# Interleaved rotary embedding on one core: two of the fifth load's sixteen positions come as fp32 over the SP queue

## The chip, the cores and the metric

The kernel runs on one core of one Trainium2 chip. The metric is the device time of one execution in microseconds, the median of several runs of the same program. Profiles are single executions taken by the hardware profiler; their times count from the start of the profiled span. The core has five engines, each with an instruction queue of its own, and they meet only at semaphores: TensorE (PE), VectorE (DVE), ScalarE (ACT), GpSimd (POOL) and SyncE (SP). TensorE isn't used here. Data moves between HBM and the on-chip memory, SBUF, by 16 DMA engines. A transfer is issued by an instruction on the POOL queue or on the SP queue; in the profile q0 (software_dynamic) carries those from POOL and q1 (hardware_dynamic) those from SP.

## The reference

`x` has the shape (8, 2048, 16, 64) in fp32: batch, sequence, heads, head dimension. `cos` and `sin` are (2048, 32). Neighbouring elements of the head dimension form a pair, and each pair is rotated by the angle of its position:

```
x_pairs = x.reshape(batch, seq_len, num_heads, head_dim // 2, 2)
x1 = x_pairs[..., 0]
x2 = x_pairs[..., 1]
out1 = x1 * cos - x2 * sin
out2 = x1 * sin + x2 * cos
out = np.stack([out1, out2], axis=-1).reshape(batch, seq_len, num_heads, head_dim)
```

All arrays are fp32. `x` and `out` have 67.1 MB each.

## The kernel before

**Tiling.** A batch `b` is one tile: 128 partitions, each with K = 16 consecutive positions, each position with 16 x 64 = 1024 elements. In HBM a partition's share is 64 KB in one piece, in SBUF 32 KB, since tiles are bf16. Loads on the POOL queue cast from fp32 to bf16 on the way, and stores on it cast back. Five tile buffers (`NX = 5`) go round for the eight batches.

**Computing.** `rotate` (L61 to L80) makes three VectorE instructions for a range of positions: `qt` = x times the sine table (L74), x = x times the cosine table in place (L75), and x = x plus `qt` with the elements of each pair swapped (L80). The tables `s_tab` and `c_tab` are bf16, made once from the raw fp32 tables by three instructions (L93 to L95); the sine table holds its sign. For `b = 0` the rotation is done in two parts, of 4 and of 12 positions; later tiles are rotated whole.

**Order.** The order on each queue is written out by hand (`manual_schedule`), and semaphores come from what each instruction reads and writes. On the POOL queue stand, one behind the other: the last 12 positions of load 0 (L85), the two raw tables (L86, L87), loads 1 to 4 (L89), store 0 (L59), the mark (L106), store 1, load 5, store 2, load 6, store 3, load 7, stores 4, 5 and 6, and the first 12 positions of store 7 (L112). Load 5 reuses tile 0's buffer and waits until store 0 has landed; loads 6 and 7 wait likewise for stores 1 and 2. The mark is a GpSimd copy of one element, position 15 of tile 4, into a place that nobody reads. It makes the POOL queue wait until load 4 has landed, before store 1 is issued.

**Both ends.** The first four positions of load 0 come in fp32 over the SP queue into `head` (L84), and ScalarE casts them into tile 0 (L91). The last four positions of store 7 are cast to fp32 by ScalarE into `tail` (L118), and SP stores them (L119). Ahead of that cast ScalarE copies one element (L117) into tile 6, which makes it wait until store 6 has landed. SP's queue thus holds two transfers, and ScalarE two casts and that copy.

**Homes.** `cos_sb` and `sin_sb`, the raw tables, have a place of their own each in the pool `consts`. `qt`, `head` and `tail` share one place in the pool `stage`.

Of the kernel before, what the change touches and what calls it, by code (L numbers as in the profile page):

```python
# [2 lines left out]

# [4 lines left out]


@with_exitstack  # L10
def kernel(
    ctx: ExitStack,
    tc: tile.TileContext,
    x: bass.AP,
    cos: bass.AP,
    sin: bass.AP,
    out: bass.AP,
):
    nc = tc.nc
    fp32 = mybir.dt.float32  # L20
    bf16 = mybir.dt.bfloat16
    mult = mybir.AluOpType.mult
    add = mybir.AluOpType.add

    B, S, H, D = x.shape
    P = 128
    K = S // P
    KP = 16
    D2 = D // 2
    HD = H * D  # L30
    NX = 5
    HEAD = 4
    TAIL = 4


    x_t = x.rearrange("b (p k) h d -> b p k (h d)", p=P, k=K)
    out_t = out.rearrange("b (p k) h d -> b p k (h d)", p=P, k=K)
    cos_t = cos.rearrange("(p k) c -> p (k c)", p=P, k=K)
    sin_t = sin.rearrange("(p k) c -> p (k c)", p=P, k=K)

    consts = ctx.enter_context(tc.tile_pool(name="consts", bufs=1))
    xpool = ctx.enter_context(tc.tile_pool(name="xpool", bufs=NX))
    stage = ctx.enter_context(tc.tile_pool(name="stage", bufs=1))

    cos_sb = consts.tile([P, K * D2], fp32)
    sin_sb = consts.tile([P, K * D2], fp32)
    c_tab = consts.tile([P, K, D], bf16)
    s_tab = consts.tile([P, K, D], bf16)

    mark = consts.tile([1, 1], bf16)  # L50
    tiles = {}

    def load(b, k0=0):
        if b not in tiles:
            tiles[b] = xpool.tile([P, K, HD], bf16, name="xt")
        nc.gpsimd.dma_start(out=tiles[b][:, k0:], in_=x_t[b, :, k0:])  # L56

    def store(b, k1=K):
        nc.gpsimd.dma_start(out=out_t[b, :, :k1], in_=tiles[b][:, :k1])  # L59

    def rotate(b, k0, k1):  # L61
        nk = k1 - k0
        xp = tiles[b][:, k0:k1]
        qt = stage.tile([P, KP, HD], bf16, name="qt", tag="work")

        def rows(a):
            return a.rearrange("p k (h e) -> p k h e", h=H, e=D)

        def tab(a):
            return dataclasses.replace(  # L70
                a, offset=a.offset + k0 * D, ap=[a.ap[0], [D, nk], [0, H], [1, D]]
            )

        nc.vector.tensor_tensor(out=rows(qt[:, :nk]), in0=rows(xp), in1=tab(s_tab), op=mult)  # L74
        nc.vector.tensor_tensor(out=rows(xp), in0=rows(xp), in1=tab(c_tab), op=mult)  # L75
        q_swap = dataclasses.replace(
            qt, offset=qt.offset + 1, ap=[qt.ap[0], [2, nk * HD // 2], [-1, 2]]
        )
        x3 = xp.rearrange("p k (a j) -> p (k a) j", j=2)
        nc.vector.tensor_tensor(out=x3, in0=x3, in1=q_swap, op=add)  # L80

    with tc.manual_schedule():
        head = stage.tile([P, TAIL, HD], fp32, name="st", tag="work")
        nc.sync.dma_start(out=head[:, :HEAD], in_=x_t[0, :, :HEAD])  # L84
        load(0, HEAD)  # L85
        nc.gpsimd.dma_start(out=cos_sb, in_=cos_t)  # L86
        nc.gpsimd.dma_start(out=sin_sb, in_=sin_t)  # L87
        for b in range(1, NX):
            load(b)  # L89

        nc.scalar.copy(out=tiles[0][:, :HEAD], in_=head[:, :HEAD])  # L91
        s2 = s_tab.rearrange("p k (i j) -> p (k i) j", j=2)
        nc.vector.tensor_copy(out=s2[:, :, 0], in_=sin_sb)  # L93
        nc.vector.tensor_scalar_mul(s2[:, :, 1], sin_sb, -1.0)  # L94
        nc.vector.tensor_copy(  # L95
            out=c_tab.rearrange("p k (i j) -> p (k i) j", j=2),
            in_=cos_sb.to_broadcast([P, K * D2, 2]),
        )
        for b in range(B):
            if b == 0:  # L100
                rotate(b, 0, HEAD)
                rotate(b, HEAD, KP)
            else:
                rotate(b, 0, KP)
            if b == 1:
                nc.gpsimd.tensor_copy(out=mark, in_=tiles[NX - 1][:1, K - 1, :1])  # L106
            if b < B - 1:
                store(b)

            if b >= 1 and b - 1 + NX < B:  # L110
                load(b - 1 + NX)
        store(B - 1, K - TAIL)  # L112

        tail = stage.tile([P, TAIL, HD], fp32, name="st", tag="work")
        nc.scalar.copy(out=tiles[B - 2][:1, 0, :1], in_=tiles[B - 1][:1, K - 1, :1])  # L117
        nc.scalar.copy(out=tail, in_=tiles[B - 1][:, K - TAIL :])  # L118
        nc.sync.dma_start(out=out_t[B - 1, :, K - TAIL :], in_=tail)  # L119


# [1 line left out]
_INS = ['x', 'cos', 'sin']  # L123
_OUTS = [((8, 2048, 16, 64), 'float32')]


# [23 lines left out]
```

## Time and profile before

| what | value |
|---|---|
| median of 3 runs | 317.34 us (317.24 to 317.46) |
| span of the profiled execution | 315.5 us |
| VectorE busy | 210.4 us, 67% of the span, 30 instructions |
| ScalarE busy | 8.6 us, 4 instructions |
| GpSimd busy | 11.9 us, 23 instructions |
| HBM read, written | 67.63 MB, 67.11 MB: 427 GB/s over the span |
| VectorE waiting for loads (L74) | 28.5 us, 3 times, the longest 12.6 |
| rotation instructions, whole tile | 8.69 us each, 7 of each line |
| casts of 128x4096 on ScalarE (L91, L118) | 3.60 us each |

A group of instructions in the profile is told by its line, engine, operation and operands, `out<-in`. The timeline gives the start and the length of each in us, and in brackets how long its engine was idle before it and what ended that. The profile counts a DMA's bytes at the place that it writes, so a casting load counts half of what it reads. A transfer's DMA work consists of packets, one for each partition's piece; with 128 partitions and 16 engines each engine has 8 of a transfer, and a completion write of 4 bytes behind them.

### The profile page before, as it was taken

What the parts mean: (1) busy time and instruction counts of PE and PEld (TensorE: products, weight loads), DVE (VectorE), ACT (ScalarE), POOL (GpSimd) and SP (SyncE); (2) the same over time, 40 slices, a digit from 0 to 9 for tenths busy, and PEclk for the clock granted to TensorE, in tenths of its full rate; (3) what the DMA queues carried; (4) which work ended last, traced back from release to release, by engine and by line L of the source; (5) the groups of instructions that cost most, each with busy time, mean ns of one, the idle gap of its engine ahead of it and who ended that gap; (6) DMA issues with size and microseconds to landing.
All of it is one profiled execution on the core that took longest, in us unless ns stands there. A gap on an engine that the chain in (4) does not pass through costs nothing.

```text
span 315.5 us, 125 instructions
## 1 busy us (share of the span) xinstructions
DVE 210.4 (67%) x30; ACT 8.6 (3%) x4; POOL 11.9 (4%) x23
## 2 busy tenths in 40 slices
DVE  0009999999999999999879960799509994000000
ACT  1030000000000000000000000000000000000400
POOL 5000000000000201010000100000000000000000
DMA  7999999999999999999999999999999999999997
GB/s 252 263 282 199 199 224 241 199 199 258 208 199 266 399 482 449 399 332 245 220 399 407 386 204 199 415 515 266 199 266 465 399 399 498 432 399 407 430 432 326
DMA packets 2752, 102.24 MB, mean 324 GB/s; under 512 B 320, under 2 KB 320, under 8 KB 448
## 3 DMA queue, kind: packets, MB, share of 16 engines
q0 software_dynamic: 2464, 98.04, 96.7%
q1 hardware_dynamic: 288, 4.19, 3.4%
HBM read 67.63 MB, written 67.11 MB: 427 GB/s over the span
## 4 chain that ended last, share of the span: by engine, by line
another core or an unknown queue 88%; DMA 5%; ACT 1%; ACTq 1%; issue 0%
DMA st<-in_x_dram 5%; ACT xt L91 1%; ACTq L145 1%; ACT xt L117 0%; ACTq L117 0%
## 5 line engine op out<-in xcount | busy, mean ns | idle before, releaser
L74 DVE TENSOR_TENSOR qt<-xt,s_tab 128x16384 bf16<-128x16384 bf16 (+2 forms) x9 | 69.7, 7743 | 28.6 <-DMA xt<-in_x_dram 28.5
L75 DVE TENSOR_TENSOR xt<-xt,c_tab 128x16384 bf16<-128x16384 bf16 (+2 forms) x9 | 69.7, 7743 | 0.4
L80 DVE TENSOR_TENSOR xt<-xt,qt 128x16384 bf16<-128x16384 bf16 (+2 forms) x9 | 69.7, 7744 | 0.3
L93 DVE CAST s_tab<-sin_sb 128x512 bf16<-128x512 f32 x1 | 0.5, 455 | 23.8 <-DMA sin_sb<-in_sin_dram 23.8
L59 POOL DMA_DIRECT2D out_dram<-xt x8 | 4.3, 533 | 129.3 <-DVE xt L80 129.3
L117 ACT COPY xt<-xt 1x1 bf16<-1x1 bf16 x1 | 0.2, 193 | 276.5 <-DMA out_dram<-xt 276.5
L56 POOL DMA_DIRECT2D xt<-in_x_dram x8 | 4.4, 575 | 73.7 <-DMA out_dram<-xt 72.9
L91 ACT CAST xt<-st 128x4096 bf16<-128x4096 f32 x1 | 3.6, 3604 | 13.3 <-DMA st<-in_x_dram 13.3
L106 POOL COPY mark<-xt 1x1 bf16<-1x1 bf16 x1 | 2.1, 2057 | 49.2 <-DMA xt<-in_x_dram 49.2
L118 ACT CAST st<-xt 128x4096 f32<-128x4096 bf16 x1 | 3.6, 3599 | 0.0
L91 ACT ACT_TABLE_LOAD x1 | 1.3, 1283 | 0.7 <-PEq L134 0.7
L95 DVE CAST c_tab<-cos_sb 128x1024 bf16<-128x1024 f32 x1 | 0.7, 683 | 0.0
L87 POOL DMA_DIRECT2D sin_sb<-in_sin_dram x1 | 0.6, 561 | 0.0
L86 POOL DMA_DIRECT2D cos_sb<-in_cos_dram x1 | 0.6, 556 | 0.0
L94 DVE TENSOR_SCALAR s_tab<-sin_sb 128x512 bf16<-128x512 f32 x1 | 0.4, 444 | 0.0
L134 POOL MEMSET const-float32-0.0<- 128x1 f32 x1 | 0.1, 98 | 0.2 <-issue 0.2
L134 POOL MEMSET const-bfloat16-1.0<- 128x1 bf16 x1 | 0.1, 101 | 0.0
L134 POOL MEMSET const-float32-1.0<- 128x1 f32 x1 | 0.1, 98 | 0.0
L134 POOL MEMSET const-uint8-127<- 128x1 uint8 x1 | 0.1, 98 | 0.0
## 6 DMA issues: line engine op xcount, KB each, us to landing
xt<-in_x_dram POOLq DMA_DIRECT2D x7, 4096.0 KB, 57.7
out_dram<-xt POOLq DMA_DIRECT2D x1, 6144.0 KB, 47.8
xt<-in_x_dram POOLq DMA_DIRECT2D x1, 3072.0 KB, 21.2
st<-in_x_dram SPq DMA_DIRECT2D x1, 2048.0 KB, 14.5
out_dram<-st SPq DMA_DIRECT2D x1, 2048.0 KB, 15.6
cos_sb<-in_cos_dram POOLq DMA_DIRECT2D x1, 256.0 KB, 21.3
sin_sb<-in_sin_dram POOLq DMA_DIRECT2D x1, 256.0 KB, 21.4
out_dram<-xt POOLq DMA_DIRECT2D x7, 70.1
```

Of the source, the lines that this page charges most:

```text
L56: nc.gpsimd.dma_start(out=tiles[b][:, k0:], in_=x_t[b, :, k0:])
L59: nc.gpsimd.dma_start(out=out_t[b, :, :k1], in_=tiles[b][:, :k1])
L74: nc.vector.tensor_tensor(out=rows(qt[:, :nk]), in0=rows(xp), in1=tab(s_tab), op=mult)
L75: nc.vector.tensor_tensor(out=rows(xp), in0=rows(xp), in1=tab(c_tab), op=mult)
L80: nc.vector.tensor_tensor(out=x3, in0=x3, in1=q_swap, op=add)
L86: nc.gpsimd.dma_start(out=cos_sb, in_=cos_t)
L87: nc.gpsimd.dma_start(out=sin_sb, in_=sin_t)
L91: nc.scalar.copy(out=tiles[0][:, :HEAD], in_=head[:, :HEAD])
L95: nc.vector.tensor_copy(out=c_tab.rearrange("p k (i j) -> p (k i) j", j=2), in_=cos_sb.to_broadcast([P, K * D2, 2]),)
L106: nc.gpsimd.tensor_copy(out=mark, in_=tiles[NX - 1][:1, K - 1, :1])
L118: nc.scalar.copy(out=tail, in_=tiles[B - 1][:, K - TAIL :])
L145: with _tile.TileContext(nc) as tc:
```

## The change

The fifth load (`b = 4`) takes only 14 of its 16 positions over the POOL queue. The last two (`FILL = 2`, 1.05 MB of fp32) come uncast over the SP queue into a new tile `fill`, and ScalarE casts them into tile 4. Ahead of that, ScalarE copies one element of tile 3's last position into `fill`, which makes SP's load wait until load 3 has landed. `fill` lies in the home of the raw tables, which become two halves of one tile `both` in a new pool `raw`; it can be written once the instructions that make the tables have read them.

```diff
+    FILL = 2
...
-    cos_sb = consts.tile([P, K * D2], fp32)
-    sin_sb = consts.tile([P, K * D2], fp32)
+    raw = ctx.enter_context(tc.tile_pool(name="raw", bufs=1))
+
+    both = raw.tile([P, 2, K * D2], fp32, name="both", tag="raw")
+    cos_sb = both[:, 0]
+    sin_sb = both[:, 1]
...
-    def load(b, k0=0):
+    def load(b, k0=0, k1=K):
         if b not in tiles:
             tiles[b] = xpool.tile([P, K, HD], bf16, name="xt")
-        nc.gpsimd.dma_start(out=tiles[b][:, k0:], in_=x_t[b, :, k0:])
+        nc.gpsimd.dma_start(out=tiles[b][:, k0:k1], in_=x_t[b, :, k0:k1])
...
-        for b in range(1, NX):
+        for b in range(1, NX - 1):
             load(b)
+        load(NX - 1, k1=K - FILL)
...
+        fill = raw.tile([P, FILL, HD], fp32, name="fill", tag="raw")
+        nc.scalar.copy(out=fill[:1, 0, :1], in_=tiles[NX - 2][:1, K - 1, :1])
+        nc.sync.dma_start(out=fill, in_=x_t[NX - 1, :, K - FILL :])
+        nc.scalar.copy(out=tiles[NX - 1][:, K - FILL :], in_=fill)
         for b in range(B):
```

The mark's own line is the same as before. The element that it reads, position 15 of tile 4, is now written by ScalarE's cast of `fill`, so in the built program the mark waits for ScalarE and no longer for load 4. The number and the order of instructions on POOL and on VectorE stay as they were; ScalarE has two more and SP one.

## The prediction

> **What bounds the kernel now.** I read the page's DMA lines first, because VectorE is busy for only 67% of the span.
>
> ```profile
> span 315.5 us, 125 instructions
> q0 software_dynamic: 2464, 98.04, 96.7%
> q1 hardware_dynamic: 288, 4.19, 3.4%
> ```
>
> The three figures behind a queue are packets, MB and the share of 16 DMA engines' span that its packets took. 96.7% and 3.4% add up to 100.1%: no engine has a pause worth naming. Next come the stretches between one transfer's first packet and the next one's (us, VectorE, ScalarE and GpSimd busy with counts, clock, DMA share, GB/s); the first is load 2, the second load 4, the others stores 0 and 1.
>
> ```profile
> 42.40:61.70 19.30, 19.20 (x4) 0.00 (x0) 0.54 (x1) 1.00 1.01 217
> 81.00:101.10 20.10, 20.03 (x3) 0.00 (x0) 0.00 (x0) 1.00 1.02 210
> 101.10:120.40 19.30, 19.23 (x3) 0.00 (x0) 2.54 (x2) 1.00 1.01 431
> 120.40:139.70 19.30, 19.13 (x4) 0.00 (x0) 1.05 (x2) 1.00 1.02 435
> ```
>
> A load writes half the bytes that a store does (bf16 against fp32), hence 217 and 431 GB/s, and takes the same 19.30 us: the fp32 side sets the price. POOL's queue is worked off in order, one transfer behind the other, 8 packets on each engine (128 rows over 16), 19.30/8 = 2.41 us a packet. Load 4 alone takes 20.10, 0.80 more than its like.
>
> Do two queues on one engine add speed? At the kernel's start the SP head and the first cast load run together; the DMA view from 5.4 to 12.7 us says:
>
> ```profile
> q0 software_dynamic: 48, 1.18, 75.2%
> q1 hardware_dynamic: 48, 0.79, 25.6%
> ```
>
> As many packets of one as of the other, and shares that add up to 100.8%: each engine takes one packet of each in turn and does one at a time. The last DMA view runs from 299 to 305.2 us; the SP store of the tail is issued at 299.11 and q1 is missing from it:
>
> ```profile
> q0 software_dynamic: 49, 2.41, 91.2%
> ```
>
> 49 is 16 engines times three, and one. So each engine began three more q0 packets after the issue before q1 had its first: a newcomer queues behind three packets already taken.
>
> Last, the timeline around the step that waits for load 4:
>
> ```profile
> 95.51 8.69 DVE L80 TENSOR_TENSOR xt<-xt,qt 128x16384 bf16<-128x16384 bf16 x1
> 102.18 2.06 POOL L106 COPY mark<-xt 1x1 bf16<-1x1 bf16 x1 [49.24 <-DMA xt<-in_x_dram]
> 104.18 0.54 POOL L59 DMA_DIRECT2D out_dram<-xt  x1
> 104.23 8.69 DVE L74 TENSOR_TENSOR qt<-xt,s_tab 128x16384 bf16<-128x16384 bf16 x1
> 112.96 8.69 DVE L75 TENSOR_TENSOR xt<-xt,c_tab 128x16384 bf16<-128x16384 bf16 x1
> 121.68 8.69 DVE L80 TENSOR_TENSOR xt<-xt,qt 128x16384 bf16<-128x16384 bf16 x1
> 122.05 0.53 POOL L56 DMA_DIRECT2D xt<-in_x_dram  x1 [17.34 <-DMA out_dram<-xt]
> ```
>
> A GpSimd copy of one element takes 2.06 us and ends at 104.24, just as VectorE's instruction ends (95.51 + 8.69 = 104.20). It seems held until VectorE changes instructions.
>
> **The change, part by part.** *Taken from q0:* 2 of 16 positions of load 4, on every row: 19.30 x 2/16 = 2.41 us of all engines. A packet of the smaller load is then 2.41 x 14/16 = 2.11 us.
>
> *Given to q1:* the same 1.05 MB as fp32, 128 rows of 8 KB, 8 on each engine. From the page, q1 moved 4.19 MB in 3.4% of 315.5 us = 10.7 us, so 2.68 us for a quarter of it. From the view of 5.4 to 12.7 us, 25.6% of 7.3 us = 1.87 us for 0.79 MB, so 2.49 us. Half-size packets may cost a little more, so I take 2.6. Net: +0.19 us, between +0.08 and +0.27. Nothing hides this, and nothing else is in its way.
>
> *Added on ScalarE:* a copy of one element when load 3 has landed, like L117 (0.19 us), and a cast of 128x2048. L91 takes 3.60 us for 128x4096; with 0.19 of it fixed, half the size is 0.19 + 3.41/2 = 1.90 us. ScalarE has nothing to do from 18.9 to 295.4, and SP's queue nothing until the tail, so neither wait holds up another instruction. VectorE's rotation of tile 4 starts at 130.4, far behind the cast. The home of the raw tables is free: their last reader, L95, ends at 25.2. The tables' own instructions keep their work and their waits. Cost 0 while the cast is done by 130.4; each us after that would first eat VectorE's 3.47 us of idle time before tile 5.
>
> *The mark on GpSimd:* it now waits for the cast, not for load 4. Behind it on POOL's queue stand store 1, load 5, store 2 and all that follows. So when does the cast end? Load 3 is seen landed at about 81.8 and the copy is done at 82.0, when SP issues. Call the small load's packets P1 to P8 on an engine, the fill's F1 to F8, store 0's S1 on. P1 begins between 80.9 and 81.5. Three more q0 packets begin after the issue, P2 to P4, so F1 comes in P5's place at 81.4 + 4 x 2.11 = 89.8 on the last engine. F1 to F4 alternate with P5 to P8: 4 x (0.32 + 2.11) = 9.7, to 99.5. I leave in the 0.80 of load 4's end: 100.3. Then F5 to F8 with S1 and S2, and S3 ahead of the completion write, since at the start q1's last write also stood behind one more q0 packet: 4 x 0.32 + 3 x 2.41 = 8.5, to 108.8. With 0.4 to be seen and 1.9 for the cast, the mark is free at 111.1. VectorE next changes instructions at 112.96, so store 1 is issued there, 8.8 us later than before. It is needed when store 0's packets run out, at 120.4 + 0.2 on the first engine: 7.6 us of cover. Cost 0. If that cover were gone, every us of delay would be a us of the end, because load 5, store 2 and the rest stand in line behind it.
>
> *Sum:* 315.5 + 0.2 = 315.7 for the profiled execution. The median, 317.34, lies 1.84 above that span; I keep the difference: **317.5 us**.
>
> [...]
>
> **The rivals.** *A. The mark misses VectorE's change at 112.96: slower.* The margin is 112.96 - 111.1 = 1.9 us. If four q0 packets and not three are ahead of the fill (SP's issue comes 1.1 us later than I reckon, after P2 has begun), all of it ends about 2.4 us later, the mark is free at 113.5, and it is held until 121.68. Store 1 is then issued at 121.7 to engines that ran dry at about 121.0. From an issue to its first packet took 1.0 us on idle engines (SP's head, 0.73 to 1.7) and at most 4.2 on POOL (issued at 1.24, q0's first packet after 5.3). So the pause is 1.7 to 4.9 us, middle 3.3: 317.5 + 3.3 = 320.8 (319.2 to 322.4). For it: the small margin, out of a row of steps each known to a few tenths. Against: A needs an error in one direction, and a mark merely 1.8 us late costs nothing. [...]
>
> *B. The fill's packets cover load 4's extra 0.80 us.* If the engines wait there for something of q0 alone, q1's packets can run meanwhile. 317.5 - 0.8 = 316.7. For: the pause is unique to this change from loads to the first store. Against: the DMA share shows no idle engine there, and a packet that holds its engine holds it for both queues.
>
> *C. The fill is free.* The change then doesn't cost q1's 2.6 us: 317.34 - 2.41 = 314.9. Against it stand the shares that add up to 100.8%.
>
> *D. Small rows cost more than the bound* (the fill's 8 KB, or the cast's 14 positions of a row): another 0.7 to 1.5 us, 318.2 to 319.0. The 24 KB packets of load 0 show no such loss: 75.2% of 7.3 us for 48 is 1.83 us each, against 2.41 x 12/16 = 1.81.
>
> **How the numbers follow.** Forecast 0.50, with its own range of 317.3 to 317.9; A 0.25; B 0.12; C 0.05; D 0.08. Below 0.2% (0.63 us, about what a measurement of this kernel can tell from none) counts as no change. The forecast and half of B (on the border, 316.71) make 0.56 for the same; the other half of B and C make 0.11 for faster; A and D make 0.33 for slower. The range from 316.6 to 320.9 holds the forecast, D, nearly all of B and somewhat over half of A: about 0.84.
>
> **What would show it.** The DMA view should have q1 at 5.24 MB and about 4.2%, and both shares again at 100% of the span. Load 4's stretch and store 0's together should be longer by 0.2 us, and all later transfers 19.30 apart. The mark should start near 111 and end at 112.96, store 1 follow it, and store 1's packets follow store 0's with no gap. A mark that ends at 121.7, and a stretch of store 0 of over 22 us, is A. A load 4 stretch without the 0.80 is B. VectorE's wait for tile 5 (160.09 before) moves by what the end moves. What would make the forecast wrong is above all the fill's first packet later than 90 us.

## The result and the profile after

The changed kernel takes 327.88 us (median of 4 runs, 327.83 to 327.91) against 317.4 us for the kernel before beside it: a ratio of 1.0332, with a 95% interval of 1.0319 to 1.0344. It is 10.5 us slower. Its profiled execution spans 326.1 us, 10.6 more than before. The same page lines as before, of the changed kernel:

```profile
span 326.1 us, 135 instructions
q0 software_dynamic: 2464, 97.52, 92.8%
q1 hardware_dynamic: 432, 5.24, 8.9%
```

q1 carries the 5.24 MB that it should, but its packets now take 8.9% of 16 engines' span, and not some 4%. The next view of the changed kernel gives the stretches of load 4, store 0, what follows it, and store 1; the last two figures are the DMA share and the GB/s, both of packets begun in the stretch.

```profile
81.00:101.15 20.15, 20.08 (x3) 0.19 (x1) 0.00 (x0) 1.00 1.01 231
101.15:120.60 19.45, 19.31 (x3) 0.00 (x0) 0.00 (x0) 1.00 1.82 433
120.60:131.48 10.88, 10.76 (x3) 1.90 (x1) 7.71 (x4) 1.00 0.00 0
131.48:150.80 19.32, 19.18 (x3) 0.00 (x0) 0.48 (x1) 1.00 1.02 436
```

Load 4 and store 0 together take 39.60 us against 39.40 before. The whole loss is the third line: behind store 0 no packet of data begins for 10.88 us. The engines' last packets end at 121.4, so all of them stand still for 10.1 us. The second line holds a riddle: a DMA share of 1.82 at an ordinary 433 GB/s. Something counts as busy there and moves nothing. The DMA view from 103.6 to 107 us has it:

```profile
q1 hardware_dynamic: 23, 0.06, 466.7%
```

In this window begin 23 packets of the fill's queue: the last 7 rows of data (0.06 MB) and 16 completion writes of 4 bytes, one for each engine. They are booked with 4.667 x 3.4 us x 16 = 254 us. The 7 rows took about 0.3 us each, so a completion write took (254 - 2)/16 = 15.7 us. In the packet records it is 16.9 or 14.5 us, begun between 103.7 and 106.9 and ended between 120.6 and 121.4, just when store 0's last packets end. The fill's data was all in at 104.5. The timeline shows what comes of it:

```profile
121.70 8.69 DVE L84 TENSOR_TENSOR xt<-xt,qt 128x16384 bf16<-128x16384 bf16 x1
121.81 1.90 ACT L109 CAST xt<-fill 128x2048 bf16<-128x2048 f32 x1 [39.85 <-DMA fill<-in_x_dram]
123.77 6.66 POOL L117 COPY mark<-xt 1x1 bf16<-1x1 bf16 x1 [70.88 <-ACT xt L109]
130.37 0.54 POOL L63 DMA_DIRECT2D out_dram<-xt  x1
```

The cast begins at 121.81, 17 us after the fill's last data. The mark starts at 123.77, in the middle of VectorE's L84, and ends with it: 121.70 + 8.69 = 130.39, and 123.77 + 6.66 = 130.43. Store 1 is issued at 130.37 in place of 104.18, and its first packet begins 1.1 us later, at 131.48. From there on all transfers are 19.3 us apart as before, so the 10.1 us go to the end undiminished.

### The profile page after: what moved, and what is told of

The parts are those of the page before. It is cut to its first block, busy times and chain, and to the rows that moved or that the text cites. A ratio compares the mean times of both kernels' runs of the same rounds, so it can differ in the third digit from the quotient of the medians.

```text
span 326.1 us, 135 instructions
## 1 busy us (share of the span) xinstructions
DVE 210.3 (64%) x30; ACT 10.7 (3%) x6; POOL 16.5 (5%) x23
## 3 DMA queue, kind: packets, MB, share of 16 engines
q1 hardware_dynamic: 432, 5.24, 8.9%
## 4 chain that ended last, share of the span: by engine, by line
another core or an unknown queue 74%; DMA 19%; ACTq 1%; ACT 1%; POOL 0%; issue 0%; PEldq 0%
DMA fill<-in_x_dram 12%; DMA both<-in_sin_dram 7%; ACTq L156 1%; ACT xt L109 1%; POOL xt L60 0%; POOL both L90 0%; ACT fill L107 0%; ACT xt L128 0%; ACTq L107 0%; ACTq L128 0%; PEldq L156 0%; ACTq L109 0%
## 5 line engine op out<-in xcount | busy, mean ns | idle before, releaser
L79 DVE TENSOR_TENSOR xt<-xt,c_tab 128x16384 bf16<-128x16384 bf16 (+2 forms) x9 | 69.7, 7743 | 0.4
L84 DVE TENSOR_TENSOR xt<-xt,qt 128x16384 bf16<-128x16384 bf16 (+2 forms) x9 | 69.7, 7743 | 0.3
L117 POOL COPY mark<-xt 1x1 bf16<-1x1 bf16 x1 | 6.7, 6660 | 70.9 <-ACT xt L109 70.9
L109 ACT CAST xt<-fill 128x2048 bf16<-128x2048 f32 x1 | 1.9, 1898 | 39.9 <-DMA fill<-in_x_dram 39.9
L100 DVE CAST c_tab<-both 128x1024 bf16<-128x1024 f32 x1 | 0.7, 681 | 0.0
## 6 DMA issues: line engine op xcount, KB each, us to landing
st<-in_x_dram SPq DMA_DIRECT2D x1, 2048.0 KB, 14.5
```

What stands on the lines that cost most here:

```text
L100: nc.vector.tensor_copy(out=c_tab.rearrange("p k (i j) -> p (k i) j", j=2), in_=cos_sb.to_broadcast([P, K * D2, 2]),)
L109: nc.scalar.copy(out=tiles[NX - 1][:, K - FILL :], in_=fill)
```

## The experiments

Theory H after this view: the fill's completion write on q1 is held while q0 carries a store to HBM; the mark turns that into lost time, and VectorE's hold on the mark (theory V) adds to it. e1 to e7 are edits of the changed kernel, and every ratio is to the kernel before, run beside them. What is said of the queues comes from the profiles of these runs; where a figure stands in no view that is shown, it comes from the times of the single packets in the run's trace.

**e1: the mark waits for load 4 again.**

```diff
-                nc.gpsimd.tensor_copy(out=mark, in_=tiles[NX - 1][:1, K - 1, :1])
+                nc.gpsimd.tensor_copy(out=mark, in_=tiles[NX - 1][:1, K - FILL - 1, :1])
```

> The mark reads position 13 of tile 4, which load 4 still brings, in place of position 15; the fill stays as it is. Theory H (the completion write of the fill on q1 is held behind store 0's writes on q0, and only the mark turns that into lost time): ScalarE's cast starts at 121 us or later just as in the changed kernel, but the mark is free at about 101.5 and ends at 104.2 with VectorE's instruction, store 1 is issued there, no stretch without packets; ratio to the kernel before 1.000 to 1.002 (317.4 to 318.0 us). Rival S (the fill itself costs the time, by small fp32 packets or by what it does to the transfers behind it): still about 327 us, ratio 1.03.

Measured: 317.51 us, ratio 1.0005 (0.9996 to 1.0015). The timeline:

```profile
102.32 2.02 POOL L117 COPY mark<-xt 1x1 bf16<-1x1 bf16 x1 [49.27 <-DMA xt<-in_x_dram]
104.28 0.54 POOL L63 DMA_DIRECT2D out_dram<-xt  x1
122.03 1.90 ACT L109 CAST xt<-fill 128x2048 bf16<-128x2048 f32 x1 [39.79 <-DMA fill<-in_x_dram]
```

The fill is seen landed just as late, at 122.03, but nothing on POOL's queue waits for it, and the time is that of the kernel before. So moving 1.05 MB to SP costs nothing that these runs can tell from zero; rival S falls. The hold also ends here at 120.9 to 121.6, although store 1's packets follow store 0's at once. It isn't let go by an idle queue.

**e2: the fill 20 us earlier, among loads only.**

```diff
-        nc.scalar.copy(out=fill[:1, 0, :1], in_=tiles[NX - 2][:1, K - 1, :1])
+        nc.scalar.copy(out=fill[:1, 0, :1], in_=tiles[NX - 3][:1, K - 1, :1])
```

> The fill waits for load 2 and not for load 3, so that it runs wholly among loads, some 20 us ahead of store 0. Theory H (held by store 0's writes): its completion write takes no longer than the head's at the start, the cast begins at about 84 to 86 us, the mark ends by 95.5, store 1 is issued before 96; ratio 1.000 to 1.002. Rival U (a completion write on q1 lands only when q0 pauses, whatever q0 carries): cast at about 121.8, mark to 130.4, ratio 1.033 as in the changed kernel.

Measured: 317.38 us, ratio 0.9998 (0.9989 to 1.0008). First the DMA view from 85.5 to 86.2 us, where the 16 completion writes begin, then the timeline:

```profile
q1 hardware_dynamic: 16, 0.00, 3.1%
```

```profile
86.58 1.90 ACT L109 CAST xt<-fill 128x2048 bf16<-128x2048 f32 x1 [23.76 <-DMA fill<-in_x_dram]
86.99 8.69 DVE L79 TENSOR_TENSOR xt<-xt,c_tab 128x16384 bf16<-128x16384 bf16 x1
88.54 7.17 POOL L117 COPY mark<-xt 1x1 bf16<-1x1 bf16 x1 [35.46 <-ACT xt L109]
95.66 0.54 POOL L63 DMA_DIRECT2D out_dram<-xt  x1
```

3.1% of 0.7 us on 16 engines is 0.35 us for all sixteen, 0.02 us each. Beside loads no hold is seen here (0.02 us), so rival U falls. The mark is held for 7.17 us by VectorE's L79 (to 86.99 + 8.69 = 95.68), and that costs nothing, since store 1 isn't needed before 120.

**e3: GpSimd only writes the mark.**

```diff
-                nc.gpsimd.tensor_copy(out=mark, in_=tiles[NX - 1][:1, K - 1, :1])
+                nc.scalar.copy(out=mark, in_=tiles[NX - 1][:1, K - 1, :1])
+                nc.gpsimd.memset(mark, 0.0)
```

> The mark's one element is first copied by ScalarE into the mark's place, and GpSimd only writes it (a memset that waits for that copy), so that GpSimd reads nothing in SBUF. Theory V (a GpSimd copy that reads SBUF is held until VectorE's two-input instruction ends; one that only writes isn't): the memset takes under 0.5 us, store 1 is issued at about 124.2 in place of 130.4, first packet about 1.1 us later; the pause of the DMA engines shrinks from 10.1 to about 4 us, 327.9 - 6.2 = 321.7 us, ratio 1.0135. Rival W (GpSimd's own cost, or any GpSimd access is held until VectorE changes instructions): 327.9 us, ratio 1.033.

Measured: 321.97 us, ratio 1.0143 (1.0127 to 1.016). The timeline:

```profile
121.93 8.69 DVE L84 TENSOR_TENSOR xt<-xt,qt 128x16384 bf16<-128x16384 bf16 x1
122.06 1.90 ACT L109 CAST xt<-fill 128x2048 bf16<-128x2048 f32 x1 [39.85 <-DMA fill<-in_x_dram]
123.99 0.19 ACT L117 COPY mark<-xt 1x1 bf16<-1x1 bf16 x1
124.25 0.09 POOL L118 MEMSET mark<- 1x1 bf16 x1 [71.11 <-ACT mark L117]
124.76 0.54 POOL L63 DMA_DIRECT2D out_dram<-xt  x1 [0.42 <-issue]
```

Writing takes 0.09 us in the middle of L84, where reading took 6.66. Store 1 is issued at 124.76, and its first packet begins at 125.87, both while L84 still runs (to 121.93 + 8.69 = 130.62): VectorE's instruction holds neither the issue nor what follows it. Rival W falls. This parts the loss, to some tenths of a us: 327.88 - 321.97 = 5.9 us come from VectorE's hold on the mark, and the remaining 321.97 - 317.4 = 4.6 us from the late completion write and the steps behind it, in which e3's second copy on ScalarE and its memset are counted too. That VectorE's instruction has two inputs, as theory V puts it, was not varied: all that held the mark here are TENSOR_TENSOR. And the opening's "only at semaphores" is too strong: in the changed kernel ScalarE's cast had let the mark go, and VectorE's instruction held it for 6.66 us.

**e4: half the fill.**

```diff
-    FILL = 2
+    FILL = 1
```

> One position of load 4 over the SP queue and not two: half the bytes, the same number of packets on q1. Theory H: the completion write is begun among store 0's packets and held to their end as before, the mark ends at 130.4 with VectorE's instruction, 327.4 to 327.9 us, ratio 1.032 to 1.033. Rival S (the cost goes with the bytes of the fill): half the loss, about 322.6 us, ratio 1.017.

Measured: 327.98 us, ratio 1.0334 (1.0318 to 1.0349). The cast is shorter (1.04 us for 1.90) and begins at 122.18; the mark starts at 123.29, takes 7.24 us and again ends with VectorE's instruction (123.29 + 7.24 = 130.53, and 121.80 + 8.69 = 130.49). Half the bytes, the same loss.

**e5: the fill 18 us later.**

```diff
-        nc.scalar.copy(out=fill[:1, 0, :1], in_=tiles[NX - 2][:1, K - 1, :1])
+        nc.scalar.copy(out=fill[:1, 0, :1], in_=tiles[NX - 1][:1, K - FILL - 1, :1])
```

> The fill waits for load 4 (position 13 of tile 4), some 20 us later than in the changed kernel, so that its data is moved beside store 0's second half. Theory H (the completion write waits for the end of the store in progress): the end of that store is what counts, so the write is held for under 5 us in place of 14.5 to 16.9 us, the cast begins at 123 to 125 us, the mark still ends with VectorE's instruction at 130.4, and the time is that of the changed kernel, 327.5 to 328.5 us, ratio 1.033. Rival L (the write takes a fixed time of some 15 to 17 us beside stores): the cast begins at about 138 us, the mark ends at 148, and the time goes to about 345 us, ratio 1.088.

Measured: 327.9 us, ratio 1.0333 (1.0314 to 1.0352). The DMA view from 120.4 to 121.1 us, when store 0 is done on every engine:

```profile
q1 hardware_dynamic: 28, 0.10, 34.4%
```

These are the fill's last 12 rows of data, 0.31 us each, and the 16 completion writes. 34.4% of 0.7 us on 16 engines is 3.85 us; less 3.72 for the rows that leaves 0.01 us for each write. The fill's data is in only at 121.1, and the cast begins at 121.45, somewhat earlier than expected. A wait of some 15 to 17 us would have put it near 138, so rival L falls as it was put. These writes began behind the store, though; for one that begins beside a store e6 is the test. The data itself isn't held: between 106 and 119 us, with store 0 going on, 76 packets of each queue begin, by turns, and a row of the fill takes 0.34 us.

**e6: store 0 in halves**, on the kernel of e3.

```diff
-    def store(b, k1=K):
+    def store(b, k1=K, k0=0):
...
-            if b < B - 1:
+            if b == 0:
+                store(b, K // 2)
+                store(b, K, K // 2)
+            elif b < B - 1:
                 store(b)
```

> The kernel with the memset mark, and store 0 issued as two transfers of 8 positions each, one behind the other on q0. Theory H (the fill's completion write is let go by the end of the transfer in progress): it lands with the first half's end at about 111 to 112 us, the cast ends by 114, store 1 is issued by 115, well ahead of 121: no pause, ratio 1.000 to 1.003 (317.4 to 318.3 us). Rival M (it lands only when store 0's writes are all through, or when q0 stops writing): as with the memset mark on the whole store, 322.0 us, ratio 1.014.

Measured: 317.59 us, ratio 1.0007 (0.9998 to 1.0016). First the DMA view from 102.7 to 104.5 us, then the timeline:

```profile
q1 hardware_dynamic: 23, 0.06, 434.0%
```

```profile
112.21 1.90 ACT L109 CAST xt<-fill 128x2048 bf16<-128x2048 f32 x1 [30.22 <-DMA fill<-in_x_dram]
...
114.39 0.09 POOL L118 MEMSET mark<- 1x1 bf16 x1 [60.91 <-ACT mark L117]
114.91 0.53 POOL L63 DMA_DIRECT2D out_dram<-xt  x1 [0.43 <-issue]
```

4.340 x 1.8 us x 16 = 125 us, less some 2 for the 7 data rows, is 7.7 us for each completion write, half of what it was. They end between 111.2 and 111.8, where the first half's last packets end and the second half's begin. So here POOL's store transfer in progress is what holds them (7.7 us for half a store, 15.7 for a whole one), and its end lets them go, though the same queue writes on without a pause. Rival M falls. Every transfer here has eight packets on each engine, so the end of the transfer and the end of eight packets that an engine took together aren't told apart.

**e7: the same fill on the POOL queue**, behind load 4.

```diff
-        nc.scalar.copy(out=fill[:1, 0, :1], in_=tiles[NX - 2][:1, K - 1, :1])
-        nc.sync.dma_start(out=fill, in_=x_t[NX - 1, :, K - FILL :])
+        nc.gpsimd.dma_start(out=fill, in_=x_t[NX - 1, :, K - FILL :])
```

> The same fill of two fp32 positions, its cast and the mark on it, but issued on the POOL queue behind load 4 and ahead of store 0, without ScalarE's copy that waits for load 3. Theory H (the two queues make the hold): the fill's completion write is done in q0's order before store 0's first packet, the cast begins at about 102.5, the mark ends at 104.2 or 113.0 with VectorE's instruction, no pause; ratio 1.000 to 1.002. Rival S (an fp32 fill and a cast behind it cost the time wherever they are issued): 322 us or more, ratio over 1.014.

Measured: 317.38 us, ratio 1.0001 (0.9992 to 1.0011). The timeline around the mark:

```profile
95.58 8.69 DVE L84 TENSOR_TENSOR xt<-xt,qt 128x16384 bf16<-128x16384 bf16 x1
102.21 1.90 ACT L108 CAST xt<-fill 128x2048 bf16<-128x2048 f32 x1 [83.25 <-DMA fill<-in_x_dram]
104.17 0.18 POOL L116 COPY mark<-xt 1x1 bf16<-1x1 bf16 x1 [51.16 <-ACT xt L108]
104.68 0.54 POOL L63 DMA_DIRECT2D out_dram<-xt  x1 [0.34 <-issue]
```

Here fp32 rows, the cast and the mark on it cost nothing that can be told from zero (ratio 1.0001), with the completion on q0 ahead of the store. The mark's copy takes 0.18 us here, because it starts 0.10 us ahead of VectorE's change at 104.27: its own work is that short, and the 2.06, 6.66 and 7.17 us elsewhere were waiting.

**e8: what load 4's extra 0.80 us is**, on the kernel before. Position 0 of batch 0 is stored from SP, out of a new fp32 tile `early`, and store 0 leaves it out.

```diff
+        k0 = 1 if b == 0 else 0
+        nc.gpsimd.dma_start(out=out_t[b, :, k0:k1], in_=tiles[b][:, k0:k1])
...
+        early = consts.tile([P, 1, HD], fp32)
...
                 rotate(b, 0, HEAD)
+                nc.scalar.copy(out=early, in_=tiles[0][:, :1])
+                nc.sync.dma_start(out=out_t[0, :, :1], in_=early)
                 rotate(b, HEAD, KP)
```

> The kernel before, with position 0 of batch 0 taken out of store 0: ScalarE casts it to fp32 when it is rotated (about 32 us), and SP stores it among the loads. Question: what the extra 0.80 us at the end of load 4 is. Theory Q (the first write into the output costs it, once): load 4's stretch shrinks to 19.3 us, and the time is 0.8 us less (316.6 us, ratio 0.9975) if the early store doesn't hold the loads up by as much itself. Rival Q2 (it belongs to the change from loads to stores on q0): the stretch keeps 20.1 us, 317.4 to 317.8 us, ratio 1.000 to 1.001. On theory H the completion writes of the loads beside the early store may land late as well; VectorE has waits of its own for load 1 at 51.8 only.

Measured: 317.34 us, ratio 1.0001 (0.9992 to 1.001). Load 4's last packets still take 3.22 us in place of 2.43 (3.36 before). It isn't the first write into the output; it stands ahead of q0's first change from a load to a store in every run here. In e7 the fill's rows stand there: they take 3.4 us on each engine, where 8 x 0.31 = 2.5 would do, and load 4's packets are as short as ever. Why only there stays open. The loads' own completion writes were not late beside this early store: load 1's took 0.01 us each, among the store's packets of 4 KB. So this store on q1 didn't hold the completion writes on q0, which the expectation had thought possible on theory H.

## Why the prediction was wrong, step by step

**What bounds the kernel** was read rightly. The DMA engines are full (96.7% and 3.4% of the span before), two queues share them by turns (in e5 76 packets of each from 106 to 119 us), and the pause on q0 is a pause of the end: 10.1 us of it, and 10.6 more of span. That the change brings no speed follows from it.

**The net cost of the moved bytes**, +0.19 us, can't be told from zero in e1 (+0.1 us) and e2 (0.0). In the changed kernel load 4 and store 0 together grew by the 0.20 us that were forecast.

**The fill's start** was reckoned too late. In the changed kernel q1's first packets come at 85.3 to 87.7 us, not 89.8: behind one or two of q0's packets, where the tail's view had three. The fill's data is thus in at 104.5. That would have helped. The prediction named a first packet later than 90 us as what would make it wrong above all; that didn't come, and it was wrong all the same.

**The step that failed** is "and S3 ahead of the completion write ... to 108.8. With 0.4 to be seen". I priced the completion write by the head's at the kernel's start, and that one lay beside a load: 0.02 us on each engine. Here the write began earlier than I reckoned, at 103.7 to 106.9, and was held for 14.5 to 16.9 us, until store 0 was through. No row of the trace before showed a completion write on q1 beside a store of q0's that was still going on: the tail's came after q0 had run dry. I took the nearest row without asking what direction its neighbour had. e2 (no store: 0.02 us), e5 (store done: 0.01 us) and e6 (half a store: half the hold) show that POOL's store in progress is the cause.

The other way round the trace before did have such a row, and it would have misled me too. The DMA view of the kernel before from 309.9 to 311.4 us, where POOL's last store ends while SP's store of the tail goes on to 314.3:

```profile
q1 hardware_dynamic: 34, 0.56, 88.6%
q0 software_dynamic: 16, 0.00, 0.6%
```

The 16 packets on q0 are the completion writes of POOL's store. 0.6% of 1.5 us on 16 engines is 0.14 us for all of them, 0.01 us each: beside this store on q1 nothing is held. So a store on the other queue was not enough for a hold here. The two cases differ in which queue the write is on, in the size of the store's rows and in that POOL's store casts; which of these matters no run here parts.

**The cover** of 7.6 us (6.5 with the 1.1 us from an issue to its first packet, which it left out) was no use, since the mark wasn't free at 111.1 but at 123.8, behind the end of store 0. The text said what that costs, each us of delay a us of the end, and so it came.

**Rival A** had the second half right: the mark that missed VectorE's change was held to the next one. It went past one change more than reckoned (121.68) to 130.4, and the pause was 10.1 us, where 1.7 to 4.9 were forecast, because what made the mark late was not a slot of 2.4 us: the fill came earlier than reckoned, not later. That A named the right direction is luck as far as that cause goes. From store 1's issue to its first packet took 1.1 us, near the lower of A's two bounds. **Rival B** falls: load 4's stretch kept its extra time with fill packets in it (20.15 us, where eight packets of 2.13 and seven rows of the fill of 0.32 make 19.3). **C** falls by e1: no gain of 2.4 us with the mark out of the way. **D** falls by e1 and e2; its 0.7 to 1.5 us were my estimate, and no run shows them.

On the length of the hold the traces show this much: the write on q1 stayed back behind packets of POOL's store that began after it, to that store's end (16.9 us at most), beside loads it didn't stay at all (0.02 us), and q0's writes didn't stay beside q1's store (0.01 us). VectorE's hold on the mark, which the prediction read from one copy of 2.06 us that ended with VectorE's instruction, is borne out by e3, where writing took 0.09 us and reading had taken 6.66, and by e7, where the copy at VectorE's change took 0.18.

## What to carry to other kernels

A small transfer on SP's queue whose completion is waited for need not finish with its data: beside a store on POOL's queue it was seen here only when that store transfer ended, in the changed kernel 17 us behind its data. The other way round, a completion on POOL's queue beside a store of SP's, nothing was held (0.01 us). So let it be through before the store begins (e2, ratio 0.9998), put it on the store's own queue ahead of it (e7, 1.0001), or cut the store (e6, 1.0007). And before a step on a queue's critical order is hung on a new event, ask which events it was safe on: here the wait for load 4 was free, and the same wait for the fill cost 10.5 us; e1, e2, e6 (with e3's mark) and e7 are four ways out of it, none faster than the kernel before, whose DMA engines were full already (96.7% and 3.4% of the span).

## What the runs showed of the hardware that was not expected

- A completion write of 4 bytes on SP's queue took 14.5 to 16.9 us beside a store of 8.39 MB on POOL's, 7.3 to 8.5 us beside one of half the size, 0.02 us beside a load, and 0.01 us with the store done. Data of both queues moved by turns beside such a store (e5, 76 packets of each from 106 to 119 us), and a completion write on POOL's queue beside a store of SP's took 0.01 us. Why the end of the transfer, and not that of the packets begun before, lets the write go is not shown by any run here.
- The last packets on q0 ahead of the first store take 0.7 to 1.1 us longer on average, in every kernel (in e7 the fill's rows, else load 4's last), and at no later change from a load to a store (2.43 us a packet ahead of stores 2, 3 and 4 in the kernel before). An earlier store from SP didn't change it (3.22 us in e8, 3.36 before).
